# Pages, priorities and queues of one residual block: where sums are kept, when gate products run, and which queue carries late transfers

## The chip, the cores and the metric

The kernel runs on one core of one Trainium2 chip. The metric is the device time of one execution in microseconds (us); lower is better. The core has engines that run side by side, each in the order its own instruction stream gives: PE (the matrix engine; its weight loads are listed as PEld), DVE (the vector engine), ACT (the scalar engine), POOL (GpSimd) and SP (the sync engine, used here to issue transfers). Transfers (DMAs) can be issued from SP, ACT or POOL. An instruction that has to wait holds up everything behind it on its engine.

## The reference

All arrays are 32-bit floats; the sequence has 512 tokens, the model width is 2048, the inner width of the feed-forward part (D_FF) is 5632. Cut to what matters:

```python
c_act = jax.nn.silu(c)
mod = c_act @ w_ada[l] + b_ada[l]
sh1, sc1, gt1, sh2, sc2, gt2 = jnp.split(mod, 6, axis=-1)
h = modulate(rms_norm(x, g_mix[l]), sh1, sc1)
proj = h @ w_in[l]
...                                  # a recurrent group and an attention group
x = x + gt1[:, None, :] * (mix @ w_out[l])
h2 = modulate(rms_norm(x, g_ffn[l]), sh2, sc2)
gate, up = jnp.split(h2 @ w_up[l], 2, axis=-1)
x = x + gt2[:, None, :] * ((jax.nn.silu(gate) * up) @ w_down[l])
```

Most of the change lies in the last three lines: the upper projection (`w_up`), the gate product `silu(gate) * up`, the lower projection (`w_down`) and the vector `gt2`, which is a matrix-vector product of `c_act` with its own 2048 columns of `w_ada`.

## The kernel before, in words

**Numbers as pairs.** Every matmul operand is split into a high part `h` and a low part `l` (`wsplit`, from L237): ACT writes the high part (L240), DVE subtracts to get the low part (L241), and PE runs three matmuls per pair of tiles, high by high, high by low and low by high (all at L245). Split weights lie in three buffers for each part, a quarter of a product's weights in each, so ACT and DVE can be at most that far ahead of PE.

**Stages in order of time.** Input projections, attention heads, the second half of the gate branch (`yr1`, hooks from L838 on), output projection (`wo`), two groups of the upper projection in plain form (`STD = 2`), then ten blocks of the upper projection in a form with seven products for a two by two split (`ORDER = (4, 5, 1, 7, 6, 2, 3)`), then the lower projection in four phases, also with seven products: 4 and 5; 1 and 7; 6; 2 and 3 (`PHASES`).

**The block loop of the upper projection (from L1167).** Each product of a block is 48 matmuls of 128 x 512. Products 4, 5 and 1 are copied out of PE's memory by ACT (L1197) into pages of the tag "c", product 7 into the tag "x", which has two buffers. After product 6 DVE forms combinations (L1204 to L1209). After product 2, and again after product 3, DVE adds the last term (L1214), ACT takes SiLU (L1217) and DVE multiplies by the other half (L1218): the gate products. Adds and copies stand in `with tc.high_priority(offset=EVAC)`, the SiLU and the multiplication in `offset=post`, where `post` is EVAC (2500) in the last block and 0 in all others. The weight sums (L1130), loads and splits stand at `AHEAD` (2000).

**What a block hands to the lower projection.** `back` (from L1156) runs inside product 5 of the next block by its place in the code: PE transposes the gate products (L1159), ACT copies the result to `uo` pages (L1162, tag "d", four buffers), and on every second feature tile `keep_act` (L1036) forms sums of an even tile `e` and an odd tile `o` on DVE (L1044 to L1047) into two fresh pages `tu` and `tw` of the tag "c", and stores five pieces to memory through SP (L1048 to L1052): that is four "c" pages a block. The tag "c" has 16 pages, but eight of them hold parts of the transformed activations through the whole block loop (`t_tags` ends with eight "c"), so eight are left for `us`, `uu`, `tu` and `tw`.

**Who sets the order.** The program is written as one stream; a planner lays out each engine's order before the run, on a clock of its own: of the instructions that are ready it takes the one that stands earliest in the code, where `high_priority(offset=n)` counts as standing n instructions earlier. It also picks the buffer for each new page from those that come free. `issue_after(i)` holds an instruction behind `i` on its engine. On the chip each engine keeps the order it was given.

**Weight sums in memory.** `sums24` (L1062) prepares sums of lower-projection weights with accumulating transfers of POOL's queue during blocks 1 to 9.

**The lower projection (from L1324).** For each quarter step `q` (0 to 10) of a phase, `dn_open` loads weights into the tags "raw" (two buffers) and "raw2" (four buffers) and the stored activation sums `td` into `tl`; `dn_prod` splits them and, for the second product, adds the two weights (L1261). All loads are issued by SP.

**The vector gt2.** Six of its 16 tiles are made earlier; the other ten are done in 40 pieces by `gt2_piece` during the lower projection: a load through ACT's queue into a "d" page (L183) and one DVE instruction with an accumulator (L194). They need a copy of `c_act` spread over all partitions, `c_b2`, which holds one "raw2" buffer until the last piece; it is loaded at step (phase, q) = (0, 1). Two pieces run at each step from (0, 2) on and so end with phase 1. `gt2_spread` at step (2, 2) writes gt2 to memory in an order that turns its 2048 numbers into 2048 pieces of four bytes (L1293), and reads it back as four broadcast pages (L1297), all through SP. `finish` uses these pages at the end of phase 2.

**Modulation blocks.** `ada1` (L479) multiplies one tile of `w_ada` by `c_act` on DVE (L161, two instructions) and asks for the next tile's load. In the stage `yr1` it stands at the steps (1, 4, 7, 10, 13) and (3, 8, 11).

Of the kernel before, what the change touches and what calls it, by code (L numbers as in the profile page):

```python
# [8 lines left out]
F32 = mybir.dt.float32  # L9
# [5 lines left out]
P = 128  # L15
# [54 lines left out]
def block_kernel(ctx, tc, xT, crow, adaT, vecs, bfr, w1, wyr, wqkv0, wqkv, wgate, wout, wup0, wups, wdn, outT):  # L70
# [404 lines left out]
    def add(hooks, n, *fns):  # L475
        hooks.setdefault(n, []).extend(fns)
        return hooks
# [326 lines left out]
    for h in range(NH):  # L804
        with tc.high_priority(offset=EVAC):
            ev = head_evac(h, ps)
        if h == 0:
            frest = forget(ps)
            make_spn()
            conv_sums()  # L810
        att = attention(h, *ev)
        att[0]()
        hk = {}
        for n, f in zip(CARRY, carry):
            add(hk, n, f)
        carry = []
        if h == 0:
            for n, f in zip(FORGET_STEPS, frest):
                add(hk, n, f)
        for n, f in zip((FIRST_STEPS if h == 0 else ATT_STEPS if h < NH - 1 else LAST_STEPS)[1:], att[1:]):  # L820
            add(hk, n, f)
        if h < 2:
            for n in range(24):
                add(hk, n * 2 // 3, lambda n=n + 24 * h: bias_in(n))
        if h == 2:
            add(hk, 1, bias_sum)
        if 2 <= h < 6:
            rp = rec_pair((2 * h - 4, 2 * h - 3))
            for n, f in zip(REC_STEPS, rp):
                add(hk, n, f)  # L830
            carry = rp[len(REC_STEPS):]
        if h >= 2:
            for n in H_ADA:
                add(hk, n, ada1)
        if h < NH - 1:
            ps = tm_group(wqkv[h], hs_, f"h{h + 1}", 384, hooks=hk)
    for n in (3, 8, 11):
        add(hk, n, ada1)  # L838
    att_rms = cp.tile([P, NT], F32, name="att_rms")
    mix = [None] * KT  # L840

# [191 lines left out]
    s2d = [drp.tile([P, 2048], F32, name=f"s2d{q}") for q in range(NQ)]  # L1033
    even = []

    def keep_act(o, f):  # L1036
        if f % 2 == 0:
            even.append(o)
            return
        e = even.pop()  # L1040
        j = f // 2
        q, ks = j // 2, slice((j % 2) * HS, (j % 2 + 1) * HS)
        u, w = page(f"tu{j}", "c"), page(f"tw{j}", "c")
        nc.vector.tensor_sub(u[:, :HS], e[:, HS:], e[:, :HS])  # L1044
        nc.vector.tensor_sub(w[:, :HS], e[:, HS:], o[:, HS:])
        nc.vector.tensor_sub(w[:, HS:], u[:, :HS], o[:, HS:])
        nc.vector.tensor_add(u[:, HS:], o[:, :HS], w[:, HS:])  # L1047
        nc.sync.dma_start(out=td[3][q][:, :, ks], in_=o.rearrange("p (a b) -> p a b", a=2))  # L1048
        nc.sync.dma_start(out=td[1][q][:, 0, ks], in_=e[:, :HS])
        nc.sync.dma_start(out=td[0][q][:, :, ks], in_=u.rearrange("p (a b) -> p a b", a=2))  # L1050
        nc.sync.dma_start(out=td[1][q][:, 1, ks], in_=w[:, :HS])
        nc.sync.dma_start(out=td[2][q][:, 0, ks], in_=w[:, HS:])  # L1052

    s4d = [drp.tile([P, 2048], F32, name=f"s4d{q}") for q in range(NQ)]
    up_loads = []
# [100 lines left out]
    def back(g, b, f, last=False):  # L1156
        pt = misc(f"up_t{b}_{f}") if last and f else rgp(f"up_t{b}_{f}")
        for t in range(NT):
            nc.tensor.transpose(out=pt[:, t * P:(t + 1) * P], in_=g[t][:, f * P:(f + 1) * P], identity=ident)  # L1159
        o = page(f"uo{b}_{f}", "d")  # L1160
        with tc.high_priority(offset=EVAC):
            nc.scalar.activation(o, pt, AF.Copy)  # L1162
        keep_act(o, 2 * STD + 4 * b + f)

    hk = {}
    nprod = halves = 0
    for b in range(NBLK):  # L1167
        un, keep_ = {}, {}
        last_block = b == NBLK - 1
        post = EVAC if last_block else 0  # L1170
        nhk = {}
        for i, p in enumerate(ORDER):
            pool = misc if (nprod + 2) % 3 == 2 else acc
            nprod += 1
            ps = [pool(f"up{b}_{p}p{t}") for t in range(2)]
            for j, hi, lo in prod_weights(p, b, un):
                th, tl = T[p][j]
                for t in range(2):
                    c_ = slice(t * P, (t + 1) * P)
                    mm(ps[t], th[:, c_], hi, j == 0, False)  # L1180
                    mm(ps[t], th[:, c_], lo, False, False)
                    mm(ps[t], tl[:, c_], hi, False, j == 7)
                for fn in hk.get((i, j), ()):
                    fn()
                if j % 4 == 3:
                    n = halves - SUMS_AT
                    halves += 1
                    if 0 <= n < SUMS_PER * NQ and n % 2 == 0 and n % SUMS_PER < 8:
                        sums24(n // SUMS_PER, n % SUMS_PER // 2)
            if b + i == 0:  # L1190
                up_last()
            if p in (4, 5, 1, 7):
                keep_[p] = []
                for t in range(2):
                    w = page(f"us{b}_{p}{t}", "c") if p != 7 else ap_.tile([P, S], F32, tag="x", name=f"us{b}_{p}{t}", bufs=2)
                    with tc.high_priority(offset=EVAC):
                        nc.scalar.activation(w, ps[t], AF.Copy)  # L1197
                    keep_[p].append(w)
            elif p == 6:
                u2 = [page(f"uu{b}_{t}", "c") for t in range(2)]  # L1200
                s4, s5, s1, s7 = (keep_[k] for k in (4, 5, 1, 7))
                with tc.high_priority(offset=EVAC):
                    for t in range(2):
                        nc.vector.tensor_add(u2[t], ps[t], s1[t])  # L1204
                for t in range(2):
                    nc.vector.tensor_sub(s7[t], u2[t], s7[t])
                    nc.vector.tensor_sub(u2[t], u2[t], s5[t])
                    nc.vector.tensor_sub(s4[t], s4[t], s7[t])
                    nc.vector.tensor_sub(s5[t], s5[t], s7[t])  # L1209
            else:  # L1210
                g, u = (s1, s4) if p == 2 else (u2, s5)
                with tc.high_priority(offset=EVAC):
                    for t in range(2):
                        nc.vector.tensor_add(g[t], ps[t], g[t])  # L1214
                with tc.high_priority(offset=post):
                    for t in range(2):
                        nc.scalar.activation(g[t], g[t], AF.Silu)  # L1217
                        nc.vector.tensor_mul(g[t], g[t], u[t])  # L1218
        hk = {(1, 1 + 2 * f): [lambda g=s1 + u2, b=b, f=f: back(g, b, f)] for f in range(4)}
# [64 lines left out]
                    mm(ps[2 * t + i], st[:, c_], w[i][part], first and n == 0, last and n == 2)  # L1284

    TAIL_AT = {(0, 1): (0, 1), (1, 0): (2, 3)}
    C_AT, GT2_AT = (0, 1), 2
    ALL = [(t, i) for t in range(2) for i in range(2)]
    gt2b = []

    def gt2_spread():
        gd = drp.tile([KT, P], F32, name="gt2d")
        nc.sync.dma_start(out=gd.rearrange("k p -> p k"), in_=mods[GT2])  # L1293
        gv = gd.rearrange("(a k) p -> a k p", k=4)
        for a in range(4):
            g = page(f"gt2b{a}", "c")
            nc.sync.dma_start(out=g.rearrange("p (k m) -> p k m", k=4), in_=gv[a:a + 1].broadcast_to([P, 4, P]))  # L1297
            gt2b.append(g)

    def finish(y, tt, a, nm, out=True):  # L1300
# [23 lines left out]
    for ph, prods in enumerate(PHASES):  # L1324
# [8 lines left out]
        for q, n in steps:  # L1333
            p = prods[n][0]
            if n == 0:
                dn_open(ph, q)
            hold = ph == 3 and q >= NQ - 2 and n == 0
            cells = dn_prod(ph, q, n, hold)
            if p not in ps:
                ps[p] = [bank(1, b, f"dn{p}p{b}") for b in range(4)]  # L1340
            if hold:
                held += cells
            for k, cell in enumerate(() if hold else cells):
                dn_mm(ps[p], *cell, ALL, q + k == 0, q == NQ - 1 and k == 1)
                if ph + n == 0 and (q, k) in TAIL_AT:
                    for f in TAIL_AT[q, k]:
                        up_tail[f]()
            if n == 0:
                if (ph, q) == C_AT:
                    gt2_c.append(bp.tile([P, 2048], F32, tag="raw2", name="c_b2"))  # L1350
                    with tc.issue_after(dn_loads[-1]):
                        nc.sync.dma_start(out=gt2_c[0], in_=c_d.broadcast_to([P, D]))
                for m in range(2 * (NQ * ph + q - GT2_AT), 2 * (NQ * ph + q - GT2_AT) + 2):
                    if 0 <= m < 4 * (KT - GT2_ADA):
                        gt2_piece(m)
                        if m == 4 * (KT - GT2_ADA) - 1:
                            gt2_sum()
                if (ph, q) == (2, 2):
                    gt2_spread()
        if ph == 0:  # L1360
            q4, q5 = copies(ps[4], "q4_"), copies(ps[5], "q5_")
# [92 lines left out]
```

## Time and profile before

| what | value |
|---|---|
| median of 3 runs | 2080.08 us (2077.1 to 2080.68) |
| time of the profiled execution | 2083.25 us |
| its span, first to last instruction | 2081.5 us |
| mean granted clock of PE | 0.989 |
| PE busy | 2034.3 us (98%) |
| DVE busy | 1678.2 us (81%) |
| ACT busy | 982.2 us (47%) |
| POOL busy | 100.1 us (5%) |

The profiled execution took 1.75 us more than its span, and 3.17 us more than the median of the runs. A row of a group reads: line, engine, operation, output<-inputs by the program's names (numbers in names left out), shapes, count | busy time, mean ns of one | idle time of the engine just before, and what ended most of it. A row of waits reads: who waited <- for whom: us in total, times, longest. In the timeline a row is start, duration, engine, line, what, and in brackets the idle time before it and what ended it. In a table of stretches the length follows the stretch, then busy time and count of each engine, the granted clock, the share of the DMA engines that was busy, and GB/s. PE's busy ends are modelled and reach into the next matmul, so lengths of stretches say more than busy time.

### The profile page before, as it was taken

What the parts mean: (1) busy time and instruction counts of PE and PEld (TensorE: products, weight loads), DVE (VectorE), ACT (ScalarE), POOL (GpSimd) and SP (SyncE); (2) the same over time, 40 slices, a digit from 0 to 9 for tenths busy, and PEclk for the clock granted to TensorE, in tenths of its full rate; (3) what the DMA queues carried; (4) which work ended last, traced back from release to release, by engine and by line L of the source; (5) the groups of instructions that cost most, each with busy time, mean ns of one, the idle gap of its engine ahead of it and who ended that gap; (6) DMA issues with size and microseconds to landing.
All of it is one profiled execution on the core that took longest, in us unless ns stands there. A gap on an engine that the chain in (4) does not pass through costs nothing. (4 is left out here: it accounts for less than half of the span.)

```text
span 2081.5 us, 25602 instructions
## 1 busy us (share of the span) xinstructions
PE 2034.3 (98%) x9329; PEld 1695.5 (81%) x9329; DVE 1678.2 (81%) x2276; ACT 982.2 (47%) x1361; POOL 100.1 (5%) x127
## 2 busy tenths in 40 slices
PE   9999999999999999999999999999999999999999
PEld 7889998888888888888787787877888777777887
DVE  8999778987897679797696786886977877886796
ACT  4433447764422266444444444444445444444443
POOL 0000001001000000000001000010000000000000
PEclk9999999999999999999999999999999999999999
DMA  9989766667689862349779956896894788888793
GB/s 350 354 299 326 245 212 224 226 211 249 239 298 322 294 214 97 100 134 265 197 175 248 256 160 177 227 279 172 229 251 127 255 269 275 282 273 269 256 329 126
DMA packets 174211, 493.97 MB, mean 237 GB/s; under 512 B 20450, under 2 KB 44930, under 8 KB 169859
## 3 DMA queue, kind: packets, MB, share of 16 engines
q1 hardware_dynamic: 158036, 445.03, 62.5%
q0 software_dynamic: 10144, 36.70, 10.4%
q10 hardware_dynamic: 5904, 10.60, 1.4%
q8 instruction: 73, 1.20, 0.2%
q14 instruction: 54, 0.44, 0.1%
HBM read 456.57 MB, written 93.36 MB: 264 GB/s over the span
## 5 line engine op out<-in xcount | busy, mean ns | idle before, releaser
L1130 DVE TENSOR_TENSOR uw<-uw,uw 128x2048 f32<-128x2048 f32 x80 | 181.9, 2283 | 0.0
L161 DVE SCALAR_TENSOR_TENSOR ada<-ada,c_b 128x1024 f32<-128x1024 f32 x108 | 131.1, 1220 | 49.1 <-DMA ada<-in_adaT 48.9
L241 DVE TENSOR_TENSOR up_2l<-uw,up_2h 128x1024 fp32r<-128x1024 f32 x70 | 85.4, 1220 | 76.4 <-ACT up_2h L240 76.3
L240 ACT ACTIVATE up_1h<-uw 128x1024 fp32r<-128x1024 f32 x70 | 74.5, 1064 | 103.6 <-PE up_7p L245 23.3
L241 DVE TENSOR_TENSOR up_1l<-uw,up_1h 128x1024 fp32r<-128x1024 f32 x70 | 85.5, 1222 | 43.4 <-ACT up_1h L240 43.0
L240 ACT ACTIVATE up_0h<-uw 128x1024 fp32r<-128x1024 f32 x70 | 74.2, 1060 | 87.1 <-PE up_5p L245 17.8
L240 ACT ACTIVATE up_3h<-uw 128x1024 fp32r<-128x1024 f32 x70 | 74.3, 1062 | 72.8 <-PE up_2p L245 16.6
L240 ACT ACTIVATE up_2h<-uw 128x1024 fp32r<-128x1024 f32 x70 | 74.1, 1059 | 70.4 <-PE up_2p L245 17.1
L241 DVE TENSOR_TENSOR up_3l<-uw,up_3h 128x1024 fp32r<-128x1024 f32 x70 | 85.4, 1220 | 17.2 <-ACT up_3h L240 16.3
L241 DVE TENSOR_TENSOR up_0l<-uw,up_0h 128x1024 fp32r<-128x1024 f32 x70 | 85.3, 1219 | 17.0 <-ACT up_0h L240 16.9
L1060 POOL DMA_DIRECT2D s2d<-in_wdn x44 | 36.5, 856 | 631.4 <-DMA s2d<-in_wdn 631.4
L245 PE MATMUL w1p<-hpl,w1h 128*128 128x512 f32 x128 | 49.8, 389 | 0.0
L245 PE MATMUL w1p<-hph,w1l 128*128 128x512 f32 x128 | 49.8, 389 | 0.0
L245 PE MATMUL w1p<-hph,w1h 128*128 128x512 f32 x128 | 42.6, 392 | 0.0
L171 DVE SCALAR_TENSOR_TENSOR ada<-ada,c_b 128x1024 f32<-128x1024 f32 x32 | 39.0, 1218 | 4.4 <-DMA ada<-in_adaT 4.4
L171 DVE SCALAR_TENSOR_TENSOR adf<-adf,c_b 128x1024 f32<-128x1024 f32 x32 | 39.0, 1219 | 0.4 <-DMA adf<-in_adaT 0.3
L1197 ACT ACTIVATE us<-up_1p 128x512 f32<-128x512 f32 x20 | 11.8, 594 | 53.1 <-DMA td<-tu 52.2
L600 ACT ACTIVATE bt<-bt,nm 128x128 f32<-128x128 f32 (+3 forms) x32 | 18.0, 561 | 39.7 <-DVE nm L598 39.4
L679 DVE SCALAR_TENSOR_TENSOR ba<-bw,sh,ba 128x512 f32<-128x512 f32 x45 | 32.6, 744 | 4.7 <-DMA bw<-in_w 3.2
L1162 ACT ACTIVATE uo<-up_t 128x512 f32<-128x512 f32 x40 | 23.6, 596 | 19.9 <-PE up_t L1159 19.9
L245 PEld LDWEIGHTS w1p<-hph,w1h 128*128 128x128 f32 x128 | 24.0, 188 | 5.4 <-issue 0.5
L245 PEld LDWEIGHTS w1p<-hph,w1l 128*128 128x128 f32 x128 | 24.0, 188 | 5.0
(2286 smaller groups left out, 6661.6 us busy)
## 6 DMA issues: line engine op xcount, KB each, us to landing
uw<-in_wups SPq DMA_DIRECT2D x160, 512.0 KB, 6.4
ada<-in_adaT SPq DMA_DIRECT2D x140, 512.0 KB, 5.5
s2d<-in_wdn POOLq DMA_DIRECT2D x44, 512.0 KB, 8.1
adf<-in_adaT SPq DMA_DIRECT2D x32, 512.0 KB, 6.2
s2d<-in_wdn SPq DMA_DIRECT2D x22, 512.0 KB, 8.9
s4d<-in_wdn SPq DMA_DIRECT2D x22, 512.0 KB, 9.7
s4d<-s2d POOLq DMA_DIRECT2D x22, 512.0 KB, 9.3
gt<-in_adaT ACTq DMA_DIRECT2D x40, 256.0 KB, 5.6
```

The source lines that it names most:

```text
L161: nc.vector.scalar_tensor_tensor(out=t, in0=t, scalar=1.0, in1=cs, op0=ALU.mult, op1=ALU.mult, accum_out=ac)
L171: nc.vector.scalar_tensor_tensor(out=t, in0=t, scalar=1.0, in1=c_b[:, cs], op0=ALU.mult, op1=ALU.mult, accum_out=ada_acc[j][:, hf, i:i + 1])
L240: tail_hi.append(nc.scalar.activation(R(hi[:, :n]), raw_ap, AF.Copy).ins)
L241: tail_lo.append(nc.vector.tensor_sub(R(lo[:, :n]), raw_ap, hi[:, :n]).ins)
L245: nc.tensor.matmul(ps, lhsT=R(l), rhs=R(r), start=start, stop=stop)
L600: nc.scalar.activation(p[:, :n], p[:, :n], AF.Exp, scale=-1.0, bias=nm, accum_out=sm)
L679: nc.vector.scalar_tensor_tensor(out=ba[j], in0=src, scalar=s1, in1=ba[j], op0=ALU.mult, op1=ALU.add)
L1060: nc.gpsimd.dma_start(out=out[:, cs], in_=src[:, cs], accum_op=ALU.add)
L1130: nc.vector.tensor_add(d_, d_, s_)
L1162: nc.scalar.activation(o, pt, AF.Copy)
L1197: nc.scalar.activation(w, ps[t], AF.Copy)
```

## The change

Five edits go together.

1. `keep_act` no longer takes "c" pages in the block loop. `tu` lies in the tag "x" (two buffers, shared with product 7's copies); the difference that went to the first half of `tw` is written over the upper half of `e`; the other half of `tw` lies in half of one page of the tag "cb", which both pairs of a block share. The four DVE instructions stay; the stores become four of the same bytes in total, the sums `tu` last.
2. The SiLU and the multiplication of the gate products stand at EVAC in every block.
3. In the last block the stores go through POOL's queue.
4. `c_b2` is loaded at step (0, 3); the pieces of gt2 start at (0, 4), two a step through phase 1, then one at each of the first four steps of phase 2. `gt2_spread` stands at step (2, 5), goes through POOL's queue, and writes in four parts.
5. The eight modulation blocks of the stage `yr1` stand at the steps 1, 3, 5, ... 15.

```diff
-            for n in H_ADA:
+            for n in H_ADA if h < NH - 1 else range(1, 16, 2):
                 add(hk, n, ada1)
...
-    for n in (3, 8, 11):
-        add(hk, n, ada1)
...
-    def keep_act(o, f):
+    w_page = []
+
+    def keep_act(o, f, late=False):
...
-        u, w = page(f"tu{j}", "c"), page(f"tw{j}", "c")
+        if j < STD:
+            u, w = page(f"tu{j}", "c"), page(f"tw{j}", "c")[:, :HS]
+        else:
+            u = ap_.tile([P, S], F32, tag="x", name=f"tu{j}", bufs=2)
+            if j % 2 == 0:
+                w_page[:] = [ap_.tile([P, S], F32, tag="cb", name=f"tw{j}", bufs=1)]
+            w = w_page[0][:, (j % 2) * HS:(j % 2 + 1) * HS]
         nc.vector.tensor_sub(u[:, :HS], e[:, HS:], e[:, :HS])
-        nc.vector.tensor_sub(w[:, :HS], e[:, HS:], o[:, HS:])
-        nc.vector.tensor_sub(w[:, HS:], u[:, :HS], o[:, HS:])
-        nc.vector.tensor_add(u[:, HS:], o[:, :HS], w[:, HS:])
-        nc.sync.dma_start(out=td[3][q][:, :, ks], in_=o.rearrange("p (a b) -> p a b", a=2))
-        nc.sync.dma_start(out=td[1][q][:, 0, ks], in_=e[:, :HS])
-        nc.sync.dma_start(out=td[0][q][:, :, ks], in_=u.rearrange("p (a b) -> p a b", a=2))
-        nc.sync.dma_start(out=td[1][q][:, 1, ks], in_=w[:, :HS])
-        nc.sync.dma_start(out=td[2][q][:, 0, ks], in_=w[:, HS:])
+        nc.vector.tensor_sub(e[:, HS:], e[:, HS:], o[:, HS:])
+        nc.vector.tensor_sub(w, u[:, :HS], o[:, HS:])
+        nc.vector.tensor_add(u[:, HS:], o[:, :HS], w)
+        eng = nc.gpsimd if late else nc.sync
+        eng.dma_start(out=td[3][q][:, :, ks], in_=o.rearrange("p (a b) -> p a b", a=2))
+        eng.dma_start(out=td[1][q][:, :, ks], in_=e.rearrange("p (a b) -> p a b", a=2))
+        eng.dma_start(out=td[2][q][:, 0, ks], in_=w)
+        eng.dma_start(out=td[0][q][:, :, ks], in_=u.rearrange("p (a b) -> p a b", a=2))
...
-        keep_act(o, 2 * STD + 4 * b + f)
+        keep_act(o, 2 * STD + 4 * b + f, last)
...
-                with tc.high_priority(offset=post):
+                with tc.high_priority(offset=EVAC):
...
-    C_AT, GT2_AT = (0, 1), 2
+    C_AT = (0, 3)
+    gt2_n = [2] * 18 + [1] * 4
...
-        nc.sync.dma_start(out=gd.rearrange("k p -> p k"), in_=mods[GT2])
+        for a in range(4):
+            nc.gpsimd.dma_start(out=gd[4 * a:4 * a + 4].rearrange("k p -> p k"), in_=mods[GT2][:, 4 * a:4 * a + 4])
...
-            nc.sync.dma_start(out=g.rearrange("p (k m) -> p k m", k=4), in_=gv[a:a + 1].broadcast_to([P, 4, P]))
+            nc.gpsimd.dma_start(out=g.rearrange("p (k m) -> p k m", k=4), in_=gv[a:a + 1].broadcast_to([P, 4, P]))
...
-                for m in range(2 * (NQ * ph + q - GT2_AT), 2 * (NQ * ph + q - GT2_AT) + 2):
-                    if 0 <= m < 4 * (KT - GT2_ADA):
-                        gt2_piece(m)
-                        if m == 4 * (KT - GT2_ADA) - 1:
-                            gt2_sum()
-                if (ph, q) == (2, 2):
+                if (ph, q) > C_AT and gt2_n:
+                    for _ in range(gt2_n.pop(0)):
+                        gt2_piece(gt2_next[0])
+                        gt2_next[0] += 1
+                    if not gt2_n:
+                        gt2_sum()
+                if (ph, q) == (2, 5):
                     gt2_spread()
```

More of the change, by code (lines that the diff above doesn't have):

```diff
@@ L1168, in block_kernel @@
         un, keep_ = {}, {}
-        last_block = b == NBLK - 1
-        post = EVAC if last_block else 0
         nhk = {}
@@ L1286, in block_kernel @@
     TAIL_AT = {(0, 1): (0, 1), (1, 0): (2, 3)}
-    C_AT, GT2_AT = (0, 1), 2
+    C_AT = (0, 3)
+    gt2_n = [2] * 18 + [1] * 4
+    assert sum(gt2_n) == 4 * (KT - GT2_ADA)
+    gt2_next = [0]
     ALL = [(t, i) for t in range(2) for i in range(2)]
```

## The prediction

> **What bounds the kernel now.** The page's head comes first, to see which engine sets the length.
>
> ```profile
> span 2081.5 us, 25602 instructions
> PE 2034.3 (98%) x9329; PEld 1695.5 (81%) x9329; DVE 1678.2 (81%) x2276; ACT 982.2 (47%) x1361; POOL 100.1 (5%) x127
> ```
>
> PE is the bound, so a change can only win where PE stands still or runs at a lower clock. The waits of PE say where, and the waits of ACT in the block loop say why.
>
> ```profile
> PE up_7p L245 <- ACT up_2h L240: 10.3, 6, 4.5
> PE dn6p L245 <- ACT dq_1w0h L240: 2.7, 1, 2.7
> PE dn6p L245 <- DVE dq_0w1l L241: 1.8, 1, 1.8
> PE dn5p L245 <- DVE dq_1w0l L241: 1.7, 1, 1.7
> ```
>
> ```profile
> ACT us L1197 <- DMA td<-tu: 52.2, 9, 9.9
> ```
>
> In six blocks PE waits inside product 7 for a split that ACT makes late. ACT itself stands 52.2 us, nine times, before the copy of product 1: that copy takes a "c" page which a store of `tu` or `tw` still reads. The splits of product 7 are queued behind it. Stretches of product 7, from its first matmul to the first of product 6, give the price; after the stretch stand its length, busy time and count of PE, weight loads and ACT, the granted clock, the DMA share and GB/s.
>
> ```profile
> 1014.86:1034.08 19.22, 14.28 (x48) 10.72 (x47) 0.49 (x1) 0.82 0.82 266
> 1101.46:1117.05 15.59, 13.02 (x48) 9.92 (x47) 0.48 (x1) 0.89 0.91 309
> 1184.40:1201.42 17.02, 14.17 (x48) 10.62 (x47) 0.48 (x1) 0.80 0.80 277
> 1268.78:1281.53 12.75, 11.44 (x48) 8.75 (x47) 0.48 (x1) 1.00 0.91 320
> 1348.94:1361.75 12.81, 11.45 (x48) 8.74 (x47) 0.48 (x1) 1.00 0.86 287
> 1429.13:1441.86 12.73, 11.45 (x48) 8.74 (x47) 0.48 (x1) 1.00 0.91 316
> 1509.24:1520.12 10.88, 10.88 (x48) 8.82 (x47) 0.48 (x1) 1.00 0.96 295
> ```
>
> A clean product 7 takes 10.88 us (the last row). The six others are longer by 8.34, 4.71, 6.14, 1.87, 1.93 and 1.85: **24.84 us**. The first three hold a lower granted clock (0.80 to 0.89) beside the gap itself. How long ACT may wait unpunished is seen from single waits:
>
> ```profile
> 1023.34 0.60 ACT L1197 ACTIVATE us<-up_1p 128x512 f32<-128x512 f32 x1 [9.87 <-DMA td<-tu]
> 1433.67 0.60 ACT L1197 ACTIVATE us<-up_1p 128x512 f32<-128x512 f32 x1 [5.92 <-DMA td<-tu]
> 1511.75 0.60 ACT L1197 ACTIVATE us<-up_1p 128x512 f32<-128x512 f32 x1 [3.92 <-DMA td<-tu]
> ```
>
> 9.87 us cost 8.34, 5.92 cost 1.85, and 3.92 cost nothing. Last, the four phases of the lower projection (busy time of PE, weight loads, DVE, ACT and POOL, then as above):
>
> ```profile
> 1631.02:1764.02 133.00, 127.12 (x545) 99.29 (x544) 107.20 (x127) 62.95 (x79) 0.00 (x0) 1.00 0.79 263
> 1764.02:1888.27 124.25, 123.13 (x529) 98.22 (x528) 102.39 (x125) 58.02 (x72) 0.00 (x0) 1.00 0.82 276
> 1888.27:1956.92 68.65, 64.07 (x265) 51.42 (x264) 39.23 (x43) 29.37 (x34) 0.00 (x0) 0.93 0.78 267
> 1956.92:2076.80 119.88, 119.88 (x529) 98.87 (x527) 99.47 (x129) 55.19 (x66) 4.43 (x8) 1.00 0.69 239
> ```
>
> The fourth is clean: 119.88 / 528 = 0.227 us a matmul. By that the third (264 matmuls, 59.94) loses 8.71 us, the second 4.37, and the first 13.1 less its 16 transposes.
>
> **The change part by part.** *Pages of their own.* In a block, product copies and `uu` need eight "c" pages and eight are free beside the activations; the four of `tu` and `tw` went on top. Without them the copy of product 1 takes pages of the last block's gate products, free once PE has transposed them. So the wait on the store goes, and the sum takes the whole **24.84**. What is late next: the copies of product 7, which now share two "x" buffers with `tu`. These fall due one product, 10.88 us, after the copies of product 1. The second pair's store of `tu` in the ninth block of ten, and the landing of all `tu` stores of the loop:
>
> ```profile
> 1509.12 0.86 SPq L1123 DMA_DIRECT2D uw<-in_wups  x2
> 1510.15 0.53 SPq L1050 DMA_DIRECT2D td<-tu  x1
> ```
>
> ```profile
> DMA to landing us min/median/max: 4.7/6.8/13.2
> ```
>
> If nothing else moved, that store, issued at 1510.15, would land at 1517.0 by the median and 1523.4 at most; product 7 ends at 1520.1 there. That is a wait of 3.3 us at most, in the part that costs nothing. The next edit makes the pair earlier still. The DVE work is the same four instructions a pair, and the stores carry the same bytes with one issue less: nothing, hidden beside PE.
>
> *Gate products at EVAC.* The product's lateness and what DVE has to do around a block's start:
>
> ```profile
> 1474.50 1.28 DVE L1214 TENSOR_TENSOR uu<-up_3p,uu 128x512 f32<-128x512 f32 x2
> ...
> 1480.28 4.49 DVE L1130 TENSOR_TENSOR uw<-uw,uw 128x2048 f32<-128x2048 f32 x2
> 1484.68 1.22 DVE L241 TENSOR_TENSOR up_0l<-uw,up_0h 128x1024 fp32r<-128x1024 f32 x1
> ...
> 1499.24 1.28 DVE L1218 TENSOR_TENSOR uu<-uu,us 128x512 f32<-128x512 f32 x2
> ```
>
> ```profile
> 1485.38 0.62 PE L245 MATMUL up_5p<-up_0h,td0h 128*128 128x512 f32 x2
> ```
>
> The last two multiplications run 24.7 us after the block's start, in product 1, so most transposes, which need them, slip from product 5 into product 1. At EVAC they come right after the adds and SiLUs, some 3 us after the start, and the transposes, `tu` and the stores move up by about 8 to 10 us. The price: 1.28 us of DVE moves ahead of the weight sums and splits. The low part of product 5's first quarter ends at 1485.9, while PE starts that product at 1485.38 and can run only two matmuls before it needs it, so there is no slack at this point. If all of it shows, that is 1.28 us in nine blocks, 11.5 in all. Against that, the second of the two sums at 1480.28 is of a later product and can slip behind the split; then it costs nothing. Most of DVE's work between a block's start and 1499 is such work ahead of need, so I take near the lower end, **2**, and keep 0 and 11.5. The SiLUs already run where they would, and the last block has had this priority all along.
>
> *Late stores and gt2 pieces in the first phase.* The first pieces stall DVE, the engine that the first phase hangs on:
>
> ```profile
> 1653.75 0.69 DVE L194 SCALAR_TENSOR_TENSOR gt<-gt,c_b 128x512 f32<-128x512 f32 x1 [2.01 <-DMA gt<-in_adaT]
> ```
>
> Two steps of the first phase lose their two pieces each: 4 x 0.69 = 2.8 us of DVE less. The stall of 2.01 us comes back at step 4, with the same cause (the load is asked for too shortly before). Eight stores leave SP, where one takes about 0.5 us (0.53 at 1510.15) between the phase's weight loads. Against it stands the 1 MB load of `c_b2`, now among the phase's own loads instead of before them. Gain 1.5, between a gain of 4 and a loss of 1.5. The second phase keeps two pieces a step: nothing.
>
> *The spread of gt2.* At the start of the third phase:
>
> ```profile
> 1881.74 0.39 SPq L1293 DMA_DIRECT2D gt2d<-mod  x1
> 1882.22 4.23 SPq L1245 DMA_DIRECT2D dq_1tl<-td  x1
> ```
>
> ```profile
> 1882.22 15.45 DMA dq_1tl<-td
> ```
>
> ```profile
> 1885.00:1896.00 11.00, 9.18 (x40) 7.17 (x38) 8.83 (x12) 2.33 (x3) 0.00 (x0) 0.96 0.37 47
> ```
>
> ```profile
> dq_5tl<-td SPq DMA_DIRECT2D x1, 256.0 KB, 5.5
> ```
>
> The load of `tl` for step 1 stands behind 2048 pieces of four bytes and takes 15.45 us instead of 5.5; for 11 us all engines together move 47 GB/s. ACT and DVE wait for it, and PE loses 2.72 us and part of a low clock. Moved three steps on and to POOL's queue, it is out of this load's way. What stays of the 8.71 us is the gap of 1.8 us, where DVE first takes eight sums out of the second phase, and perhaps one stretch of low clock. The second row of product 7 has gaps of 15.59 - 13.02 = 2.6 us and loses 0.11 x 15.59 = 1.7 us to its clock; for one gap of 1.8 I take half of that, 0.9, between 0 and 1.7.
>
> In the new place the 2048 writes meet other loads. I take 2.5 us for that, between nothing and 7.5: a `tl` load late by 15.45 - 5.5 = 10 us, less the 5 us or so that splits run ahead, plus a low clock. So the phase loses 1.8 + 0.9 + 2.5 = 5.2 instead of 8.7: gain **3.5**, between 6.9 and a loss of 2. The four single pieces (0.69 us of DVE each) and the "raw2" buffer held four steps longer lie under a phase in which DVE is busy 39.23 of 68.65 us.
>
> *Modulation blocks in `yr1`.* The same eight; two of 2.4 us now fall near the end of the stage instead of one. What waits there:
>
> ```profile
> PE wo0p L245 <- DVE mx2l L234: 0.5, 1, 0.5
> ```
>
> ```profile
> DVE ada L161 <- DMA ada<-in_adaT: 11.1, 7, 3.6
> ```
>
> PE's 0.5 us wait for DVE could grow by up to 2.4, and DVE's waits for these tiles could shrink and take the gap away. I take 0, between a gain of 1 and a loss of 2.4.
>
> **Sum.** -24.84 + 2 - 1.5 - 3.5 + 0 = -27.8. The profiled execution took 2083.25, so the change would make it 2055.4; it stood 3.17 above the median of the runs, so against the median: 2080.08 - 27.8 = **2052**.
>
> **The rivals.** *DVE becomes the bound at each block's start.* The multiplications show in full in nine blocks: 9.5 more than I took, 2062. For it: no slack at 1484.68. Against it: the 4.49 us of sums in front that can slip.
>
> *The spread stalls every queue.* The writes of four bytes hold up the engines themselves, so the other queue helps nothing and the stall hits `tl` loads in mid-phase: the phase's gain of 3.5 goes, 2056. For it: 47 GB/s over 11 us. Against: in that stretch all transfers sat in one queue. The Trainium skill's page "DMA: Bandwidth & Descriptors", section "Issuing engines are not separate DMA queues", holds with this rival: transfers of SP, ACT and GpSimd run on the same 16 engines, and another issuer saves issue time only. No run here shows small writes in one queue beside loads in another.
>
> *The wait stays.* The planner gives the copies of product 1 pages that come free no sooner: only the 5.0 of the lower projection remain, 2075, or 2077 with the 2 of DVE. Against it: the releaser in all nine waits is the store, which "c" pages would no longer see.
>
> *Slower: the wait goes to product 7.* If the `tu` store, now last of the four, is put behind a weight load that waits for its buffer, the "x" buffers come free late. It has happened in the third block, whose product 7 ended at 1034.08:
>
> ```profile
> 1022.25 0.53 SPq L1050 DMA_DIRECT2D td<-tu  x1
> ```
>
> On a clean clock that product 7, begun at 1014.86, would have ended at 1025.74. With the longest landing, 13.2 us, the store is done 9.7 us after that, with one of 10 us 6.5 after. In the middle, 8.1 us, and on the line between 5.92 (1.85) and 9.87 (8.34), a block loses 5.4 us, nine blocks 49: 2052 + 49 = 2101. It decides from a wait of about 6.7 us on, where nine blocks at 3.1 eat the gain. Against it: the store is held there by the very stall that goes, and in the ninth block it goes out 0.9 us after product 7's start (1510.15 against 1509.24), not 7.4.
>
> **How the numbers follow.** The forecast has 0.62, with its own range 2043 to 2061; DVE at the block's start 0.12 (2062); the spread 0.11 (2056); the wait that stays 0.06 (2077); the wait at product 7 0.09 (2101). The low end is all gains at their best: 24.84 + 4 + 6.9 + 1 = 36.7, 2043. The high end is 24.84 - 11.5 - 1.5 - 2.4 = 9.4 with the third phase at no gain: 2071. That leaves out the last two cases and 0.04 below. A measurement of this kernel can tell 0.2%, 4 us, from no change: the first three cases and a little are faster, 0.86; the wait that stays is the same within that, 0.05; slower 0.09.
>
> **What would show it.** Right: no wait of `us` on `td`, all ten stretches of product 7 at 10.88 and clock 1.00, transposes in product 5; the third phase near 65 us and the first near 131. Wrong: new waits of ACT before L1197 at product 7, PE waiting on `up_0l` in product 5, a `tl` load of over 10 us in the third phase, or a product 7 that is still long.

## The result, and the profile after

The changed kernel takes **2064.38 us** (median, 2061.89 to 2065.66), beside 2079.02 us for the kernel before on the same chip: a ratio of 0.9928, 95% interval 0.9911 to 0.9946. That is 14.6 us faster; the forecast of 2052 had 28 us. The profiled executions stand 19.8 us apart (2083.25 and 2063.41), because that of before lay above its median and that of after below; the stages below are compared in those. All times of parts are read from one execution each, and the 820 us ahead of the block loop differ from one execution to the next by up to 7 us even where the code there is the same, so stages are compared one by one and whole times by their medians.

The head of the page after, which answers the one quoted in the prediction:

```profile
span 2061.7 us, 25611 instructions
PE 2023.9 (98%) x9329; PEld 1695.8 (82%) x9329; DVE 1676.4 (81%) x2276; ACT 985.0 (48%) x1361; POOL 111.3 (5%) x143
```

PE is still the bound and does the same 9329 matmuls and transposes, in 10.4 us less; the rest of the gain is gaps. Stretches of the trace, by the same columns as in the prediction (stretch, length, busy PE, weight loads, DVE, ACT, POOL, granted clock, DMA share, GB/s). First the block loop of before, not shown so far:

```profile
825.73:1631.02 805.29, 790.98 (x3506) 646.46 (x3504) 641.42 (x621) 378.01 (x439) 54.55 (x66) 0.99 0.72 200
```

Then, of after, the block loop, the third block's product 7 (19.22 us before) and the four phases of the lower projection:

```profile
826.35:1605.01 778.66, 778.66 (x3506) 645.08 (x3505) 640.06 (x621) 381.51 (x439) 54.50 (x66) 1.00 0.75 207
...
1015.11:1025.99 10.88, 10.88 (x49) 9.01 (x48) 4.90 (x4) 5.33 (x7) 0.00 (x0) 1.00 1.04 391
...
1605.01:1733.83 128.82, 125.83 (x546) 99.62 (x544) 104.89 (x119) 62.94 (x79) 5.35 (x8) 1.00 0.78 264
1733.83:1857.69 123.86, 122.97 (x529) 98.24 (x528) 101.83 (x121) 58.52 (x73) 0.00 (x0) 1.00 0.81 278
1857.69:1934.30 76.61, 65.50 (x265) 52.04 (x263) 39.51 (x53) 27.18 (x32) 5.23 (x8) 0.91 0.92 226
1934.30:2056.78 122.48, 121.95 (x528) 100.00 (x528) 102.05 (x131) 56.53 (x68) 4.33 (x8) 0.99 0.71 249
```

| Stage | before | after | change | forecast |
|---|---|---|---|---|
| ahead of the block loop | 825.7 | 826.4 | +0.6 | 0 |
| block loop | 805.3 | 778.7 | **-26.6** | -22.8 |
| first phase | 133.0 | 128.8 | -4.2 | -1.5 |
| second phase | 124.3 | 123.9 | -0.4 | 0 |
| third phase | 68.7 | 76.6 | **+8.0** | -3.5 |
| fourth phase | 119.9 | 122.5 | +2.6 | 0 |

The block loop is now all PE: length and busy time are equal, the clock is 1.00, and all ten products 7 take 10.88 us (one 10.87). ACT's waits ahead of its copies into `us`, which had 52.2 us for stores of `tu`, in the loop after:

```profile
ACT us L1201 <- PE up_7p L245: 9.8, 10, 1.0
ACT us L1201 <- PE up_1p L245: 9.6, 10, 1.0
ACT us L1201 <- PE up_5p L245: 8.7, 9, 1.0
ACT us L1201 <- PE up_4p L245: 8.2, 9, 0.9
```

These are all: the copies wait for their own products, not for a store. The two phases around the spread of gt2, the third and the fourth, gave 10.6 us back. The waits of PE from 1862 to 1942 us, and those of ACT from 1866 on, say on what:

```profile
PE dn6p L245 <- ACT dq_7w0h L240: 6.3, 1, 6.3
PE dn2p L245 <- ACT dq_0w0h L240: 2.6, 1, 2.6
PE dn6p L245 <- DVE dq_0w1l L241: 1.8, 1, 1.8
```

```profile
ACT dq_7th L1261 <- DMA dq_7tl<-td: 10.4, 1, 10.4
ACT dq_0th L1261 <- DMA dq_0tl<-td: 7.7, 1, 7.7
ACT dq_6th L1261 <- DMA dq_6tl<-td: 4.9, 1, 4.9
```

The 1.8 us are the gap at the phase's start that was there before. The 6.3 and the 2.6 are new: ACT cannot split because `tl` loads of SP's queue are late, and PE runs dry twice, once in the third phase and once at the start of the fourth. The chain of waits has the load on it:

```profile
1884.42 20.55 DMA dq_7tl<-td
```

Such a load took 5.5 us undisturbed in the kernel before. What is in flight at that time is the spread of gt2. POOL's instructions in order of time, and then the stretches between them:

```profile
1879.33 0.79 POOL L1301 DMA_DIRECT2D gt2d<-mod  x1 [255.83 <-DVE mod L201]
1892.23 0.77 POOL L1301 DMA_DIRECT2D gt2d<-mod  x1 [12.11 <-issue]
1905.08 0.75 POOL L1301 DMA_DIRECT2D gt2d<-mod  x1 [12.08 <-issue]
1917.66 0.76 POOL L1301 DMA_DIRECT2D gt2d<-mod  x1 [11.83 <-issue]
```

```profile
1879.30:1892.20 12.90, 12.90 (x59) 10.68 (x58) 5.29 (x5) 3.80 (x5) 0.79 (x1) 1.00 1.07 184
1892.20:1905.10 12.90, 7.81 (x34) 5.81 (x32) 3.05 (x3) 2.54 (x4) 0.79 (x2) 0.89 0.94 187
1905.10:1917.70 12.60, 11.03 (x36) 8.43 (x36) 6.19 (x6) 5.21 (x7) 0.77 (x2) 0.70 1.06 238
```

POOL stands some 12 us before each further write of 512 pieces, held by nothing that the profile shows, so the four writes follow one another from 1879.3 to about 1930. For two thirds of the phase all transfers together move 184 to 238 GB/s. ACT lacks its data, PE is busy for 7.81 us out of 12.90, and then runs 12.6 us at a clock of 0.70.

### The profile page after: what moved, and what is told of

Read it like the earlier page. It is cut to its first block, busy times and chain, and to the rows that moved or that the text cites. A ratio compares the mean times of both kernels' runs of the same rounds, so it can differ in the third digit from the quotient of the medians.

```text
span 2061.7 us, 25611 instructions
## 1 busy us (share of the span) xinstructions
PE 2023.9 (98%) x9329; PEld 1695.8 (82%) x9329; DVE 1676.4 (81%) x2276; ACT 985.0 (48%) x1361; POOL 111.3 (5%) x143
## 5 line engine op out<-in xcount | busy, mean ns | idle before, releaser
L308 POOL TENSOR_TENSOR ss<-ss,mhalf 128x8 f32<-128x8 f32 x8 | 15.1, 1882 | 268.3 <-DVE ss L307 186.8
L245 PEld LDWEIGHTS w1p<-hpl,w1h 128*128 128x128 f32 x128 | 24.0, 188 | 5.0
```

Of the source, the lines that this page charges most:

```text
L245: nc.tensor.matmul(ps, lhsT=R(l), rhs=R(r), start=start, stop=stop)
L308: nc.gpsimd.tensor_tensor(out, mean, mhalf[:, :out.shape[-1]], ALU.pow)
```

## The experiments

**Pages alone and priority alone.** Two theories of the block loop: the forecast's (pages bring nearly all, the priority costs DVE time), and that DVE becomes the bound at each block's start. One run has the new `keep_act` with the old priority, the other only this:

```diff
-                with tc.high_priority(offset=post):
+                with tc.high_priority(offset=EVAC):
                     for t in range(2):
                         nc.scalar.activation(g[t], g[t], AF.Silu)
```

> The kernel before with the first edit alone (sums in pages of their own). If the wait of ACT on the store is a matter of the pages, product 7 is at 10.88 us in all ten blocks and the time is about 24 us under the kernel before, 2055. If the pages only pass the wait on to the copies of product 7, because the transposes still come in product 1, ACT waits there some 1 to 5 us a block and product 7 or 6 stays long in some blocks: 2058 to 2070.

> The kernel before with the second edit alone (gate products at evaluation priority). The stores then go out about 10 us earlier; the longest wait of ACT was 9.9 us, of which some 5 cost nothing. If lateness alone was the cause, this edit removes the loss by itself: about 2055. If the pages are the cause, waits of a few us and part of the loss remain: 2060 to 2070. If DVE at a block's start were the price, product 5 would be 1.28 us longer in each block: up to 11.5 us of the gain gone.

Pages alone: 2055.69 us, ratio 0.9887 (0.9866 to 0.9908). Priority alone: 2062.9 us, ratio 0.9912 (0.9883 to 0.994). Both are against a median of 2080.4 us. The block loop with pages alone:

```profile
823.02:1604.20 781.18, 781.18 (x3505) 641.59 (x3504) 642.74 (x621) 380.56 (x439) 54.47 (x66) 1.00 0.74 206
```

The block loop with the priority alone, its third block's product 7, and the releasers of the copies into `us`:

```profile
823.31:1610.05 786.74, 780.77 (x3505) 644.49 (x3504) 638.99 (x621) 379.24 (x439) 54.48 (x66) 1.00 0.74 204
...
1012.07:1026.07 14.00, 11.48 (x50) 8.93 (x48) 4.72 (x4) 5.58 (x7) 0.00 (x0) 1.00 0.98 305
```

```profile
ACT us L1197 <- DMA td<-tw: 25.4, 6, 6.6
ACT us L1197 <- DMA td<-tu: 5.0, 3, 3.3
```

Pages alone take 24.1 us off the loop (805.29 to 781.18), the priority alone 18.5, both together 26.6: they are two remedies for the same wait. The priority moves the multiplications and with them the stores forward, so the copies wait 30.4 us in all instead of 52.2, and most of those waits are short enough to cost little. Beside the pages it brings the last 2.5 us (781.18 to 778.66): with the pages alone 14 of a block's 16 transposes run in product 1 and products 5 and 1 take 23.93 us together, with both edits all 16 run in product 5 and the two take 23.66, in nine blocks. The DVE instructions moved ahead cost PE nothing: product 5 takes 12.66 us with its 16 transposes, as much as product 1 took with 14 (12.65). What the forecast named as late next does show, with the pages alone:

```profile
ACT us L1205 <- DMA td<-tu: 5.2, 4, 2.2
```

Four copies wait for a store of `tu`, those of product 7 in the "x" buffers, 2.2 us at most, where the prediction had 3.3 at most and no cost; PE has no wait in this loop either. With the priority beside the pages this wait is gone too. That DVE becomes the bound is refuted: PE has no wait at all in the loop after.

The first run shows something else: pages alone, at 2055.69 (2054.49 to 2058.18), are faster than the whole change, at 2064.38 (2061.89 to 2065.66). Something in the rest costs more than it brings.

**The spread in other queues and forms.** Is it the new place, the queue, the cut into four, or the four-byte pieces? On the changed kernel the spread was issued in one piece by SP at its new place; in four parts by SP; and with gt2 turned by PE first, so that it is written from 16 partitions in rows of 512 bytes, by SP. In all three SP also issues the four transfers that read gt2 back. The first and the last as diffs, without the lines of the reads:

```diff
-        for a in range(4):
-            nc.gpsimd.dma_start(out=gd[4 * a:4 * a + 4].rearrange("k p -> p k"), in_=mods[GT2][:, 4 * a:4 * a + 4])
+        nc.sync.dma_start(out=gd.rearrange("k p -> p k"), in_=mods[GT2])
...
```

```diff
-        for a in range(4):
-            nc.gpsimd.dma_start(out=gd[4 * a:4 * a + 4].rearrange("k p -> p k"), in_=mods[GT2][:, 4 * a:4 * a + 4])
+        pt = acc("gt2t")
+        nc.tensor.transpose(out=pt[:KT, :P], in_=mods[GT2], identity=ident)
+        gs = small(P, "gt2s", 1)
+        with tc.high_priority(offset=EVAC):
+            nc.vector.tensor_copy(out=gs[:KT, :], in_=pt[:KT, :P])
+        nc.sync.dma_start(out=gd, in_=gs[:KT, :])
...
```

> The changed kernel with the spread of gt2 in one piece on SP's queue, still at step (2, 5). Theory A: what costs is that POOL's queue carries the 2048 writes as four transfers of 12 us one after the other; then one transfer leaves one hole of some 11 us, the third phase falls from 76.6 us to 66 to 70, the fourth to 120, and the time is 2053 to 2058. Theory B: writes of four bytes in the middle of the phase cost the same from any queue: third phase 74 to 79 us, time 2062 to 2067.

> The changed kernel with gt2 turned by one transpose on PE and written from 16 partitions in rows of 512 bytes, all on SP's queue; no writes of four bytes. By both theories the third phase has no hole left: 62 to 63 us (59.9 and the 1.8 us gap at its start with its clock), the fourth 120, the time about 2064.4 - 14 - 2.6 = 2048. If loads are still late in the third phase, the writes were not the cause.

> The changed kernel with the spread on SP's queue, still in four parts of 512 writes. Theory A1: the four parts cost because POOL's queue takes one at a time and each lasts 12 us; on SP the four follow each other like the one piece, some 3 us each: third phase 66 to 69 us, fourth 120. Theory A2: any transfer of such writes lasts 12 us, however many there are; then four cost 48 us on SP too, with SP's own loads behind them: third phase 75 us or more.

One piece by SP: 2049.67 us, ratio 0.9855 (0.9835 to 0.9874). Rows: **2044.18 us, ratio 0.9827 (0.9807 to 0.9847)**. Four parts by SP: 2049.1 us in one execution. The third phase with one piece by SP, and the stretch in which its write is in flight:

```profile
1859.05:1926.62 67.57, 63.98 (x266) 51.63 (x264) 42.25 (x55) 29.28 (x33) 0.00 (x0) 0.95 0.83 280
...
1890.70:1902.90 12.20, 12.20 (x55) 10.12 (x54) 5.50 (x5) 4.29 (x5) 0.00 (x0) 1.00 0.56 118
```

The third phase with four parts by SP, and with rows:

```profile
1854.88:1922.56 67.68, 62.32 (x266) 50.50 (x264) 42.16 (x55) 28.95 (x33) 0.00 (x0) 0.97 0.98 271
```

```profile
1852.57:1914.68 62.11, 60.29 (x266) 49.49 (x265) 42.13 (x56) 29.18 (x33) 0.00 (x0) 1.00 0.90 304
```

The write's issue, number and size, with the median time to landing, first with one piece by SP, then with four parts by SP, then in the changed kernel:

```profile
gt2d<-mod SPq DMA_DIRECT2D x1, 8.0 KB, 12.2
```

```profile
gt2d<-mod SPq DMA_DIRECT2D x4, 2.0 KB, 12.0
```

```profile
gt2d<-mod POOLq DMA_DIRECT2D x4, 2.0 KB, 12.4
```

A write of 512 pieces is not faster in SP's queue: beside loads it lands after 12.0 us (the last of the four after 16.0), and 2048 pieces in one write land after 12.2. So theory A1 has the length of the phase right, but not its "some 3 us each"; and A2 has the 12 us of one write right, but not the 48 of four: SP issues its four within 5.5 us and they are in flight together, all landed 21.5 us after the first issue, where POOL's four follow one another over 50.7 us. This is what the change of queue cost, 9 us of the third phase (the reads, which moved with it, do no harm in POOL's queue, as the run with rows there shows below). The cut into four itself left the phase as long on SP (67.68 against 67.57), though PE waits 3.5 us behind the writes instead of 1.8, because there is less of a low clock (0.97 against 0.95).

Even so, one piece by SP at the new place, 67.6 us, is hardly better than the 68.65 of the kernel before: the write stalls the loads in mid-phase as it did at the start, 118 GB/s over 12 us, and PE pays a little later (1.2 and 0.5 us, and the clock). With the spread by SP at its old place the phase takes 67.85 to 68.65 in the executions on record, one of them of the changed kernel (the old gt2, below), so the new place is worth 0.2 to 1.1 us. The time of the first run, 2049.67, lies below the 2053 to 2058 of theory A, whose length of the phase it has.

With rows the phase is clean but for the known 1.8 us gap (62.11 against 59.94 for its matmuls), and the fourth phase is back at 119.9. This kernel beats the two with the spread by SP.

**POOL's queue: its price, by form and by number.** Three theories: POOL's queue is slow beside SP's loads whatever it carries; each issue has a price; each piece has a price. Rows, but issued by POOL:

```diff
-        nc.sync.dma_start(out=gd, in_=gs[:KT, :])
+        nc.gpsimd.dma_start(out=gd, in_=gs[:KT, :])
...
-            nc.sync.dma_start(out=g.rearrange("p (k m) -> p k m", k=4), in_=gv[a:a + 1].broadcast_to([P, 4, P]))
+            nc.gpsimd.dma_start(out=g.rearrange("p (k m) -> p k m", k=4), in_=gv[a:a + 1].broadcast_to([P, 4, P]))
```

> The changed kernel with gt2 turned by PE and written from 16 partitions in rows of 512 bytes, but all five transfers of the spread in POOL's queue. 'Small pieces': the four-byte pieces are what held the loads up, POOL's queue does no harm by itself; the write lands within some 7 us, the third phase is 62 to 64 us as with the rows in SP's queue, about 2044 us. 'POOL's queue': a transfer in it is slow beside SP's loads whatever its form; the third phase stays at 70 us or more, 2052 us or more.

2049.19 us in one execution (beside it, before took 2087.63, above all its other runs). The third phase:

```profile
1858.86:1922.59 63.73, 61.91 (x267) 50.63 (x265) 42.13 (x56) 29.17 (x33) 2.71 (x5) 0.97 0.86 300
```

No `tl` load is late, and PE waits for nothing but the known gap; the phase differs from the 62.11 above only by a low clock, and it took the same 63.73 in another kernel with rows by SP (the stores in SP's queue, below). The whole time missed the expected 2044. Against the profiled execution with rows by SP (2040.92) it is 8.3 us longer: 1.6 in this phase and 6.4 ahead of the block loop, which the edit doesn't touch. That part here, and with the rows in SP's queue:

```profile
0.00:827.63 827.63, 807.61 (x3962) 699.01 (x3962) 686.70 (x1234) 397.87 (x674) 41.59 (x53) 0.99 0.76 262
```

```profile
0.00:821.23 821.23, 805.56 (x3962) 697.81 (x3963) 686.56 (x1234) 397.83 (x674) 42.08 (x53) 1.00 0.77 264
```

So POOL's queue does no harm with rows in it. Then the four-byte pieces in eight writes of 256 instead of four of 512:

```diff
-        for a in range(4):
-            nc.gpsimd.dma_start(out=gd[4 * a:4 * a + 4].rearrange("k p -> p k"), in_=mods[GT2][:, 4 * a:4 * a + 4])
+        for a in range(8):
+            nc.gpsimd.dma_start(out=gd[2 * a:2 * a + 2].rearrange("k p -> p k"), in_=mods[GT2][:, 2 * a:2 * a + 2])
```

> The changed kernel with its spread in POOL's queue cut into eight writes of 256 pieces where there were four of 512. 'A price for each issue': every write takes the 12.4 us that it took with 512 pieces, eight of them 99 us from 1879 on, so the last ends near 1978, 43 us after the third phase; the final sums of that phase wait and the time is 2090 us or more. 'A price for each piece': each takes about half, some 6 us, the eight end near 1929 as the four did, and the time stays within 2055 to 2070 us.

2064.01 us in one execution. POOL's writes in order of time:

```profile
1879.94 2.15 POOL L1301 DMA_DIRECT2D gt2d<-mod  x3 [254.98 <-DVE mod L201]
1892.00 2.13 POOL L1301 DMA_DIRECT2D gt2d<-mod  x3 [9.92 <-issue]
1905.81 1.43 POOL L1301 DMA_DIRECT2D gt2d<-mod  x2 [11.68 <-issue]
```

Neither theory fits as it was put. Three writes of 256 go out at once, then POOL stands until some 12 us have passed, and so on: three turns of 12 to 14 us with 768, 768 and 512 pieces, where the changed kernel had four turns of 12.5 with 512. So the price is one for each turn, and how much goes into a turn is limited. The third phase stays at 77.52 us.

Last, whether a turn is slow by itself or only beside loads: at the start of the block loop, where next to no transfer runs, four times 512 pieces more, written to memory that nobody reads.

```diff
+            if (gi, f) == (1, 0):
+                qd = drp.tile([KT, P], F32, name="qd")
+                for a in range(4):
+                    nc.gpsimd.dma_start(out=qd[4 * a:4 * a + 4].rearrange("k p -> p k"), in_=t2[:, 4 * a:4 * a + 4])
```

> The changed kernel with one thing more: at the start of the block loop, where for 20 us hardly any transfer runs (1 GB/s from 820 to 840 us), POOL's queue also writes four times 512 pieces of four bytes from a page that is ready at about 827 us to memory that nobody reads. 'The pieces are slow by themselves in that queue': each write takes about 12 us here too, 50 us together. 'They are slow because each waits for the loads of SP's queue on the shared engines': the writes that run before the loads begin at 849 us take well under 12 us each, some 3 us (128 us of piece time in SP's queue made 2048 pieces in 12.2 us, a quarter of it for 512), and all four are done before 849. The time is 0 to 10 us above that of the changed kernel.

2063.79 us in one execution. (No run shows the 128 us in the expectation's brackets; its 3 us are a quarter of SP's 12.2.) POOL's instructions, then three stretches of this kernel, then the last two of them in the changed kernel without the extra writes:

```profile
828.21 0.94 POOL L1089 DMA_DIRECT2D qd<-su  x1 [66.58 <-DVE su L1085]
838.74 0.77 POOL L1089 DMA_DIRECT2D qd<-su  x1 [9.58 <-issue]
847.98 0.75 POOL L1089 DMA_DIRECT2D qd<-su  x1 [8.47 <-issue]
858.36 0.76 POOL L1089 DMA_DIRECT2D qd<-su  x1 [9.63 <-issue]
```

```profile
828.20:838.70 10.50, 10.50 (x48) 8.71 (x47) 10.45 (x9) 4.94 (x6) 0.94 (x1) 1.00 0.02 0
...
849.30:858.40 9.10, 9.10 (x42) 7.54 (x41) 8.00 (x14) 6.06 (x9) 0.04 (x1) 1.00 0.66 13
858.40:870.00 11.60, 11.60 (x53) 9.62 (x52) 5.80 (x5) 5.49 (x7) 0.71 (x1) 1.00 1.02 201
```

```profile
849.30:858.40 9.10, 9.10 (x42) 7.54 (x41) 8.00 (x13) 5.61 (x9) 0.00 (x0) 1.00 0.74 216
858.40:870.00 11.60, 11.60 (x53) 9.62 (x52) 5.47 (x5) 5.92 (x7) 0.00 (x0) 1.00 0.83 272
```

With nothing beside it a turn of 512 pieces lasts 9 to 10.5 us, not 3: the pieces are slow by themselves in that queue, and loads add only some 2 us. (No run has such a write in SP's queue without loads, so whether they are slow by themselves there too is open.) And they hold up the other queue: SP's loads, issued from 849.7 on (849.2 without the extra writes), move 13 GB/s until 858.4 instead of 216, though their packets count as in flight for 0.66 of the time. The hold is not whole in every turn: during the fourth, 858.4 to 870, 201 GB/s move instead of 272. PE waits for none of these loads, so the loop stays at 778.65 us.

**The rest, undone one at a time.** On the kernel with rows, the last block's stores back in SP's queue (`keep_act` without `last`); on the changed kernel, `c_b2`, the pieces of gt2 and the spread as before; on the changed kernel, the steps in `yr1` as before.

> The kernel with gt2 written in rows (e4_rows), and the last block's stores back on SP's queue. If the late stores on POOL's queue make the first phase's gain, its 128.7 us go up by 1.5 to 2.8; if the gain is that the gt2 pieces start two steps later, it stays at 128.5 to 129.2.

> The changed kernel with gt2 as in the kernel before: c_b2 at (0, 1), two pieces a step from (0, 2), spread by SP at (2, 2) in one piece. First phase: 130.5 to 132 if the pieces make the gain there, near 129 if the stores do. Third phase as before the change, 68 to 69 us, so that the move of the pieces and of the spread is worth about 1 us there on SP's queue.

> The changed kernel with the modulation blocks of yr1 at their old steps. The stretch from yr1's first matmul to the second output group took 103.3 us before (495.05 to 598.31) and 104.7 after (492.63 to 597.33), of which a part is a low clock. If the new steps cost DVE time at the end of the stage, it falls by 0.5 to 2 us; if not, it stays within 0.5 of 104.7 less what the clock does.

Each is one execution. Stores in SP's queue: 2044.37 us, the same as 2044.18. Old gt2: 2052.57. Old `yr1`: 2064.46, the same as 2064.38; its stretch from `yr1` to the second output group takes 105.2 us, against 104.7 in the changed kernel at the same clock of 0.98, so the new steps cost nothing there. The first phase with the stores in SP's queue, and with the old gt2, where DVE's wait for a piece's load is given too:

```profile
1601.11:1730.18 129.07, 125.43 (x546) 99.69 (x544) 104.95 (x119) 62.96 (x79) 0.00 (x0) 1.00 0.79 265
```

```profile
1600.60:1734.36 133.76, 128.27 (x545) 100.47 (x544) 107.38 (x127) 62.81 (x79) 5.35 (x8) 0.99 0.77 262
```

```profile
DVE gt L194 <- DMA gt<-in_adaT: 4.1, 2, 2.5
```

The stores' queue is worth nothing that shows (129.07 against 128.74 with rows). The later pieces and the later load of `c_b2` are worth 4.9 us here (133.76 to 128.82), more than the expected 1.5 to 3: DVE has eight instructions and 2.5 us of work less, and 4.1 us of waits for the first pieces' loads go. In all profiled executions the first phase takes 131.6 to 133.9 us with the old pieces (four kernels) and 128.1 to 129.7 with the new (nine). The whole old treatment of gt2, at 2052.57, is still faster than the new one in POOL's queue, because the third phase then takes 67.85 us and the fourth 119.91.

## Why the prediction was right and where it was off

The measured 2064.38 lies in the range (2043 to 2071) and on the side that had 0.86. The likeliest value, 2052, was 12 us too low. In profiled executions the forecast made 2055.4 and the trace has 2063.41: 8 us, with errors of both signs in it.

- **Pages of their own, 24.84:** right. Alone they took 24.1 us off the loop, with the whole change the wait of `us` on `td` is gone, and ten products 7 stand at 10.88 us. The rivals that the wait stays (2077) or goes to product 7 (2101) are refuted.
- **Gate products at EVAC, +2:** sign wrong, and below the bound of 0. DVE had enough work ahead of need to let the multiplications through, and with the transposes whole in product 5, products 5 and 1 came out 2.5 us shorter in nine blocks; why 16 together cost PE less than 2 and 14 is not shown. The rival that DVE becomes the bound (2062) lies 2 us from the result, but it is not what happened.
- **First phase, -1.5:** mis-sized, measured -4.2, just beyond the bound of 4. The later pieces and the later `c_b2` alone brought 4.9; the stores brought nothing that shows.
- **The spread of gt2, -3.5 in the third phase:** this is **the step that failed**. Its term "I take 2.5 us for that, between nothing and 7.5" was far too small: the third phase loses 16.7 us (76.61 less 59.94) where the prediction had 5.2, so with the 1.8 and the 0.9 as it put them the term is 14.0, beyond its own bound, and the fourth phase loses 2.6 more. The wrong premise is that the writes would make a `tl` load late once, by the 10 us seen in SP's queue. In POOL's queue 512 pieces last as long as 2048 did in SP's, and they come four times, each only after the one before, so the disturbance lasts 50 us of a 77 us phase and reaches into the next. Even the part that moved them off the phase's start was worth 0.2 to 1.1 us only, not 3.5: in SP's queue at the new place the phase takes 67.57.
- **`yr1`, 0:** right; undone, it changes nothing that shows.

The rival "the spread stalls every queue" named the mechanism but priced it as no gain in the third phase; what was missing was the fourfold length. Its sentence from the Trainium skill, page "DMA: Bandwidth & Descriptors", section "Issuing engines are not separate DMA queues", is borne out in so far as the other queue is no way around the pieces: SP's loads fall from 216 to 13 GB/s while another issuer's pieces are in flight. That another issuer saves issue time only leaves out what happened here: with the same four writes the third phase takes 76.61 us from POOL and 67.68 from SP. The result thus landed near two rivals by an error of 11.5 + 2.6 us in one term, against gains of 3.8 and 2.7 beyond the forecast in two others. Without these two gains it would be 2071, the upper end of the range; that it lies well inside is luck in part.

## What to carry to other kernels

Before moving a transfer of many tiny pieces to another queue to get it out of the way, ask how long it lasts there and what it holds up; turning it into long rows first (here one transpose by PE and one copy by DVE) removed the disturbance, and the choice of queue then no longer mattered. Two edits that shorten the same wait don't add up (24.1 and 18.5 made 26.6), so price each of them beside the other. When a change has several parts, time its main part alone: here it beat the whole.

## What the runs showed of the hardware that was not expected

- 512 pieces of four bytes through POOL's queue last 9 to 10.5 us alone and 12.4 us beside loads; beside loads, SP's queue takes 12 to 16 us for as many and 12.2 for 2048 in one write. The queues differ in what is in flight together: SP had four such writes at once, while POOL's next write waits until the one before is through; with writes of 256 pieces three go out together in one such turn. While a turn runs alone, the DMA engines show a busy share of 0.02, so it isn't the moving of the bytes that lasts; what it is, is not settled. The Trainium skill, page "DMA: Bandwidth & Descriptors", section "Anatomy of one DMA — SWDGE (gpsimd) path", gives 2.0 us and the bytes over 436 GB/s for a transfer of this path, thus an estimate of 2.0 us for 2 KB; the measurement decides, and for four-byte pieces it is some five times that.
- The gap of 1.8 us at the start of the third phase was followed by a low clock in some executions (63.73 us at 0.97, twice) and by none in another (62.11 at 1.00), with rows in all three and the same 1.8 us of waiting. What decides it, no run shows. The 0.9 us that the prediction took for it is a mean of two cases.
